# Attention weights of block b+1 beside the values of block b, and the softmax division after P V

## The chip, the cores and the metric

The kernel runs on one core of one Trainium2 chip. The time is device microseconds of one execution of the whole program, the median of several runs. TensorE appears in the profile as PE (matmuls) and PEld (its weight loads), VectorE as DVE, ScalarE as ACT, GpSimd as POOL, and SyncE's DMA queue as SP. Each engine works through its own list of instructions strictly in order; engines wait for each other on semaphores.

## The reference

Two layers (DEPTH = 2) of a decoder trunk over 512 tokens of width 1024. In each layer a norm feeds one projection whose columns are divided among three mixers (sparse attention, an S5 state space, a Mamba-2 SSD), whose outputs go through one output projection, and then a squared-ReLU MLP of width 4096 follows. The part that the change touches is the end of the attention:

```python
logits = jnp.einsum('bqgrd,bqkgd->bqgrk', qg, k_sel).astype(jnp.float32) * ATTN_SCALE
logits = jnp.where(valid[:, :, None, None, :], logits, -jnp.inf)
p = jax.nn.softmax(logits, axis=-1).astype(v_sel.dtype)
o = jnp.einsum('bqgrk,bqkgd->bqgrd', p, v_sel)
```

There are 8 query heads of width 64 in 2 groups of 4 (each group shares its keys and values), and the queries are taken in 4 blocks of 128. Each query keeps at most 128 keys, chosen by an indexer (512 // 4, `topk`).

## The kernel before

Everything lies as columns of tokens: 128 partitions, 512 tokens or 128 keys along the free dimension. The big products are made from two parts, a high and a low one, with three matmuls each (`mm3`, lines 458 to 460); the weights are cut into `whi` on ACT (L191) and `wlo` on DVE (L192) as they arrive.

A layer has two stages. In `mixers` eight or more generators (streams) run side by side: `trunk_in` (input projection), `keys` (key transposes and indexer scores), `select` (top-k masks), `attention`, two `recurrent` streams (S5 and SSD), and three `out_proj` streams (S5's, then attention's, then SSD's part of the output projection). `merge` advances the stream whose own clock is lowest; each `yield` tells how much the step adds to that clock, and tables in `PLAN` scale these steps (`pace`), delay a stream's start (`start`), add to its priority (`prio`) and name the PSUM pool of each tile (`bank`: `m` and `a`, four banks each). The order in which the instructions then stand on each engine is made by the scheduler of the tile framework from these priorities and from buffers as they come free. In `mlp` the second stage runs, nearly alone.

The names that matter, with the lines of the profile:

- `attention` (from L1305) goes through the blocks b = 0 to 3. For each it turns the queries (`rope_q`), splits and transposes them (`hhl` L1042/1043, `hTp` L1046, `hT` L1048), waits for the block's mask, and runs `attend`.
- `attend` (from L1092) makes, for each of 8 heads, the scores `lg` on PE (L1055), the masked scores and their row minimum on DVE (`pe`, `nmax`, L1107), and the exponential with its row sum on ACT (L1108). After four heads it takes the reciprocal of the four sums (L1111) and multiplies each of the four weight tiles by it: head 0 on ACT (L1115, since `norm_act` is (0,)), the other three on DVE (L1117). Then, for each block of keys, four weight tiles of a group are transposed on PE (`pTp`, L1123), copied out of PSUM by ACT (`pT`, L1125) and multiplied by the values (`po`, L1128, 64 output partitions for each group). At the end the four rows of `po` are cut into `mh` (ACT, L1132) and `ml` (DVE, L1133), the operands of the output projection.
- A block's 8 heads and all of its transposes and products with the values are done before the next block's queries are touched.
- Around it run the SSD's steps: `xb` (L1210), the convolution `cv` (L844 to 851), `CT` (L857/858), `ssdT` (L880), `ssds` (L893), `ssdy` (L907/909), `st` (L914), and top-k's `mx`/`isc` (L1086/1087) with the mask's last step (L1090).

Of the kernel before, what the change touches and what calls it, by code (L numbers as in the profile page):

```python
# [10 lines left out]
F32 = mybir.dt.float32  # L11
F32R = mybir.dt.float32r
I32 = mybir.dt.int32
AF = mybir.ActivationFunctionType
ALU = mybir.AluOpType
# [3 lines left out]
P = 128  # L19
# [3 lines left out]
NB = S // P  # L23
# [24 lines left out]
    "serial": "no",  # L48
    "norm_act": (),
    "tab_dve": (),  # L50
# [3 lines left out]
    "prio": {},  # L54
# [9 lines left out]
        "serial": "no",  # L64
        "norm_act": (0,),
        "tab_dve": ("B1", "C2"),
        "pace": {"w": 0.29, "key": 2.007, "idx": 0.686, "top": 0.061, "q": 3.616, "att": 1.702, "s5": 0.084, "ssd": 2.496, "out": 1.504, "tab": 0.3},
        "start": {"tab": 0.5, "key": 5.0, "top": 41.0, "att": 0.0, "s5": 12.0, "ssd": -7.0, "out": 20.0},
        "prio": {"att": 300, "idx": -30, "top": -300, "ssd": 300, "tab": -30, "w": 30, "s5": 30, "out": -30, "q": -300},
        "bank": {"w_kv": "m", "w_qi": "m", "w_q": "m", "w_u5": "m", "w_xa": "a", "w_xb": "m", "w_z": "m", "kT": "a", "hT": "a", "ix": "a", "lg": "a", "pT": "m", "po": "a", "sB": "m", "sst": "a", "sU": "a", "sv": "m", "sy": "m", "st": "m", "sg": "a", "dds": "a", "dseg": "m", "darow": "m", "dT": "a", "ds": "a", "dy": "a", "dst": "a", "dn": "a", "db": "m"},  # L70
    },
# [4 lines left out]
        "serial": "no",  # L76
        "norm_act": (0,),
        "tab_dve": (),
        "pace": {"w": 0.344, "key": 1.011, "idx": 1.036, "top": 0.873, "q": 3.741, "att": 1.652, "s5": 0.357, "ssd": 1.82, "out": 0.453, "tab": 0.853},
        "start": {"tab": 0.0, "key": 0.0, "top": 15.0, "att": -20.0, "s5": -30.0, "ssd": 3.0, "out": 22.0},  # L80
        "prio": {"tab": -30, "out": -100, "att": 1000, "q": -300, "idx": -30, "s5": 1000, "top": -100},
        "bank": {"w_kv": "m", "w_qi": "m", "w_q": "m", "w_u5": "m", "w_xa": "a", "w_xb": "m", "w_z": "m", "kT": "a", "hT": "a", "ix": "b", "lg": "a", "pT": "a", "po": "a", "sB": "m", "sst": "a", "sU": "m", "sv": "m", "sy": "a", "st": "b", "sg": "a", "dds": "a", "dseg": "m", "darow": "m", "dT": "m", "ds": "m", "dy": "a", "dst": "a", "dn": "a", "db": "m"},
    },
# [137 lines left out]
class Net:  # L221
# [869 lines left out]

    def attend(self, b, qT, K, mask, nrs, ah, al):  # L1092

        nc = self.nc
        v = nc.vector
        nk = (b + 1) * P
        po = self.ps(self.bank["po"], (P, 4, P), name="po")
        es = []
        for g_ in range(2):
            sm = self.s([P, 4], tag="psum", bufs=4)  # L1100
            for r in range(4):
                p = self.ps(self.bank["lg"], name="lg")[:, :nk]
                self.head_dot(p, qT[2 * r + g_], K, g_, nk)
                e = self.g(name="pe")[:, :nk]
                nm = self.s([P, 1], tag="nmax", bufs=8)
                h = 2 * r + g_
                v.tensor_tensor_reduce(e, p, mask, nrs[:, h:h + 1], 3.0e38, ALU.add, ALU.min, nm)  # L1107
                nc.scalar.activation(e, e, AF.Exp, bias=nm, scale=-1.0, accum_out=sm[:, r:r + 1])  # L1108
                es.append(e)
                yield self.pace["att"] * (0.4 + 0.25 * b)  # L1110
            v.reciprocal(sm, sm)  # L1111
            for r in range(4):
                e = es[4 * g_ + r]
                if r in self.plan["norm_act"]:
                    nc.scalar.activation(e, e, AF.Copy, scale=sm[:, r:r + 1])  # L1115
                else:
                    v.tensor_scalar(e, e, sm[:, r:r + 1], None, ALU.mult)  # L1117
        for kb in range(b + 1):
            pts = []
            for g_ in range(2):  # L1120
                p = self.ps(self.bank["pT"], (P, 4, P), name="pTp")
                for r in range(4):
                    nc.tensor.transpose(p[:, r], es[4 * g_ + r][:, kb * P:(kb + 1) * P], self.ident)  # L1123
                pt = self.g([P, 4, P], name="pT")
                nc.scalar.activation(pt, p, AF.Copy)  # L1125
                pts.append(pt)
            for g_ in range(2):
                nc.tensor.matmul(po[g_ * 64:g_ * 64 + 64], self.vt[:, kb, g_], pts[g_], start=kb == 0, stop=kb == b)  # L1128
            yield self.pace["att"] * 2.2
        bs = slice(b * P, (b + 1) * P)  # L1130
        for r in range(4):
            nc.scalar.activation(ah[r][:, bs], po[:, r], AF.Copy)  # L1132
            v.tensor_tensor(al[r][:, bs], po[:, r], ah[r][:, bs].bitcast(F32), ALU.subtract)  # L1133

# [170 lines left out]
    def attention(self, l, r):  # L1305
        nc = self.nc
# [3 lines left out]
        q, rt = r["q"], self.rt  # L1310
# [8 lines left out]
        al = [self.g(dt=F32R, name="ml") for _ in range(4)]  # L1319
        for b in range(NB):  # L1320
            self.rope_q(q[b], *rt[2][b])
            qT = self.transpose_heads(q[b])
            yield self.pace["q"] * 2.5
            while b not in r["mask"]:
                yield None
            yield from self.attend(b, qT, r["K"], r["mask"][b], qrs[:, b], ah, al)
        for i in range(4):
# [254 lines left out]
```

## Time and profile before

| | us |
|---|---|
| median of 3 runs | 1332.54 (1331.55 to 1332.56) |
| the profiled execution | 1328.87 |
| its span in the trace | 1327.1 |
| PE busy | 1218.0 (92%) |
| DVE busy | 885.2 (67%) |
| ACT busy | 549.2 (41%) |
| layer 0, mixers / MLP | 0 to about 340 / 340 to 708 |
| layer 1, mixers / MLP | 708 to about 986 / 986 to 1327 |

The blocks of attention run between about 140 and 295 us (layer 0) and between about 842 and 935 us (layer 1). A busy PE in this profile is not a PE at its peak, and PEclk is the clock that was granted, as a share of full speed (1.0 is 2.4 GHz, 0.5 is 1.2 GHz). In a wait that ends for several reasons, the profile names the last one.

### The profile page before, as it was taken

How to read it: one execution, taken by the hardware profiler on the slowest of the kernel's cores; microseconds unless marked ns; L12 is line 12 of the kernel's file. 1: busy time of each engine (PE TensorE's matmuls, PEld its weight loads, DVE VectorE, ACT ScalarE, POOL GpSimd, SP SyncE). 2: the span in 40 equal slices, each digit the busy share in tenths (PEclk: the TensorE clock that was granted, in tenths of full speed). 3: DMA queues.
4: the chain of work that ended last, by engine and by line, in shares of the span. 5: the costliest groups of instructions: out<-in, count | busy, mean ns of one | idle time of the engine just before them, and what ended most of it. 6: DMA issues, size and time to landing. Idle time of an engine off the chain costs nothing.

```text
span 1327.1 us, 17056 instructions
## 1 busy us (share of the span) xinstructions
PE 1218.0 (92%) x5708; PEld 977.1 (74%) x5708; DVE 885.2 (67%) x2024; ACT 549.2 (41%) x1128; POOL 169.7 (13%) x302
## 2 busy tenths in 40 slices
PE   5678957889999989999999989968999999999998
PEld 5566745458888868888888767754788888888887
DVE  5998999857886545665564699975475445444443
ACT  4245444664543533534443234455254233242331
POOL 2385100000796040000000000000000000000000
PEclk9889988899999999999999989978999999999999
DMA  5132220002567647677644634300323333333332
GB/s 189 40 88 70 74 74 24 9 1 72 148 213 257 214 146 252 224 262 230 227 149 137 219 120 124 120 17 1 111 88 97 101 97 96 96 96 99 100 110 81
DMA packets 139688, 161.64 MB, mean 122 GB/s; under 512 B 18768, under 2 KB 107600, under 8 KB 139600
## 3 DMA queue, kind: packets, MB, share of 16 engines
q1 hardware_dynamic: 139600, 160.55, 38.5%
q8 instruction: 45, 0.74, 0.2%
q14 instruction: 43, 0.35, 0.1%
HBM read 128.29 MB, written 31.03 MB: 120 GB/s over the span
## 4 chain that ended last, share of the span: by engine, by line
PE 62%; DVE 19%; issue 7%; POOL 6%; ACT 4%; DMA 1%; SPq 0%; ACTq 0%; DVEq 0%; POOLq 0%
PE pm L458 18%; PE pm L460 18%; PE pm L459 18%; PE po L1128 3%; DVE isc L1087 2%; DVE mx L1086 2%; DVE isc L1076 2%; PE pTp L1123 1%; DVE pe L1107 1%; DVE wlo L192 1%; DMA wraw<-in_w_in_dram 1%; POOL pt L660 1%; DVE cv L847 1%; ACT pe L1108 1%; POOL pt L661 1%
## 5 line engine op out<-in xcount | busy, mean ns | idle before, releaser
L192 DVE TENSOR_TENSOR wlo<-wraw,whi 128x512 fp32r<-128x512 f32 (+1 forms) x312 | 223.2, 718 | 243.0 <-ACT whi L191 241.4
L191 ACT ACTIVATE whi<-wraw 128x512 fp32r<-128x512 f32 (+1 forms) x312 | 194.1, 625 | 374.5 <-PE pm L459 236.9
L458 PE MATMUL pm<-xh,whi 128*128 128x512 f32 x640 | 252.4, 395 | 3.8 <-ACT q L1224 3.2
L460 PE MATMUL pm<-xh,wlo 128*128 128x512 f32 x640 | 250.1, 392 | 1.2 <-DVE wlo L192 1.2
L459 PE MATMUL pm<-xl,whi 128*128 128x512 f32 x640 | 250.9, 392 | 0.0
L460 PE MATMUL pm<-uh,wlo 128*128 128x512 f32 x512 | 199.7, 390 | 0.3 <-DVE wlo L192 0.3
L458 PE MATMUL pm<-uh,whi 128*128 128x512 f32 x512 | 199.6, 390 | 0.0
L459 PE MATMUL pm<-ul,whi 128*128 128x512 f32 x512 | 199.6, 390 | 0.0
L458 PEld LDWEIGHTS pm<-xh,whi 128*128 128x128 f32 x640 | 120.8, 189 | 30.8 <-ACT q L1224 3.9
L460 PEld LDWEIGHTS pm<-xh,wlo 128*128 128x128 f32 x640 | 120.6, 189 | 27.4 <-DVE wlo L192 2.0
L459 PEld LDWEIGHTS pm<-xl,whi 128*128 128x128 f32 x640 | 121.1, 189 | 24.2 <-issue 0.2
L460 PEld LDWEIGHTS pm<-uh,wlo 128*128 128x128 f32 x512 | 96.2, 188 | 20.8 <-DVE wlo L192 0.9
L459 PEld LDWEIGHTS pm<-ul,whi 128*128 128x128 f32 x512 | 96.3, 188 | 20.4 <-issue 0.4
L458 PEld LDWEIGHTS pm<-uh,whi 128*128 128x128 f32 x512 | 96.2, 188 | 20.3 <-issue 0.4
L458 PE MATMUL pm<-whi,xh 128*128 128x512 f32 (+1 forms) x176 | 67.4, 385 | 14.0 <-ACT xh L392 12.8
L460 PE MATMUL pm<-whi,xl 128*128 128x512 f32 (+1 forms) x176 | 66.6, 380 | 1.3 <-DVE xl L394 1.3
L459 PE MATMUL pm<-wlo,xh 128*128 128x512 f32 (+1 forms) x176 | 67.0, 381 | 0.5 <-DVE wlo L192 0.3
L1408 DVE TENSOR_TENSOR ul<-ur,uh 128x512 fp32r<-128x512 f32 x64 | 48.5, 758 | 21.0 <-ACT uh L1407 21.0
L1406 DVE SCALAR_TENSOR_TENSOR ur<-pm,ur 128x512 f32<-128x512 f32 x64 | 43.9, 686 | 23.0 <-ACT ur L1403 22.7
L1414 DVE TENSOR_TENSOR sq<-pm,r2b 128x512 f32<-128x512 f32 x64 | 44.1, 689 | 17.5 <-PE pm L460 17.5
L1407 ACT ACTIVATE uh<-ur 128x512 fp32r<-128x512 f32 x64 | 39.9, 624 | 30.7 <-DVE ur L1406 30.7
L1087 DVE MATCH_REPLACE8 isc<-mx,isc 128x256 f32<-128x256 f32 (+2 forms) x96 | 51.6, 541 | 0.0
(345 smaller groups left out, 1931.4 us busy)
## 6 DMA issues: line engine op xcount, KB each, us to landing
wraw<-in_w_up_dram SPq DMA_DIRECT2D x128, 256.0 KB, 2.8
wraw<-in_w_down_dram SPq DMA_DIRECT2D x128, 256.0 KB, 2.8
st<-shi SPq DMA_DIRECT2D x48, 256.0 KB, 2.9
st<-slo SPq DMA_DIRECT2D x48, 256.0 KB, 3.5
wlo<-st SPq DMA_DIRECT2D x48, 256.0 KB, 3.0
whi<-st SPq DMA_DIRECT2D x48, 256.0 KB, 2.8
wraw<-in_w_in_dram SPq DMA_DIRECT2D x32, 256.0 KB, 2.8
sraw<-in_w_in_dram SPq DMA_DIRECT2D x32, 256.0 KB, 3.9
```

What stands on the lines that cost most here:

```text
L191: nc.scalar.activation(hi, raw, AF.Copy)
L192: nc.vector.tensor_tensor(lo, raw, hi.bitcast(F32), ALU.subtract)
L458: nc.tensor.matmul(p, lh, rh, start=first, stop=False)
L459: nc.tensor.matmul(p, lh, rl, start=False, stop=False)
L460: nc.tensor.matmul(p, ll, rh, start=False, stop=last)
L1076: v.scalar_tensor_tensor(acc, r, wi[:, h:h + 1], acc, ALU.mult, ALU.add)
L1087: v.match_replace(acc, m8, acc, SENT)
L1128: nc.tensor.matmul(po[g_ * 64:g_ * 64 + 64], self.vt[:, kb, g_], pts[g_], start=kb == 0, stop=kb == b)
L1406: v.scalar_tensor_tensor(r, p, 0.0, r, ALU.max, ALU.mult)
L1407: nc.scalar.activation(h, r, AF.Copy)
L1408: v.tensor_tensor(lo, r, h.bitcast(F32), ALU.subtract)
L1414: v.tensor_tensor(t, d[1], rb, ALU.mult)
```

## The change

Three things change together.

1. `attend` is cut in two generators. `weights` makes the scores, exponentials and row sums of a block (the sums of all 8 heads now in one tile, 128x8); `values` does the transposes and the products with the values. `attention` starts `values` of block b together with `weights` of block b+1 and advances them in turn, weights first. The queries of block b+1 are turned and transposed before `values` of block b starts.
2. The weights aren't divided by their sums any more: L1111, L1115 and L1117 go (`norm_act` with them). The reciprocals of all 8 sums are taken in one instruction in `values`. Eight matmuls of 128x128 identity columns against the reciprocal, broadcast to 64 columns, write the reciprocals into a PSUM tile `rsb` with the layout of `po` (64 partitions for a group, one row for each r); ACT copies it to `rn`. After the last `po` DVE multiplies `po` by `rn`, a 128x512 instruction.
3. `mh` and `ml` are cut from `rn` in SBUF and not from `po` in PSUM.

`rsb` lies in pool `m` in layer 0 and in pool `a` in layer 1.

```diff
-    def attend(self, b, qT, K, mask, nrs, ah, al):
+    def weights(self, b, qT, K, mask, nrs, es, sm):
 ...
-        po = self.ps(self.bank["po"], (P, 4, P), name="po")
-        es = []
         for g_ in range(2):
-            sm = self.s([P, 4], tag="psum", bufs=4)
             for r in range(4):
 ...
-                nc.scalar.activation(e, e, AF.Exp, bias=nm, scale=-1.0, accum_out=sm[:, r:r + 1])
+                nc.scalar.activation(e, e, AF.Exp, bias=nm, scale=-1.0, accum_out=sm[:, g_, r:r + 1])
                 es.append(e)
                 yield self.pace["att"] * (0.4 + 0.25 * b)
-            v.reciprocal(sm, sm)
-            for r in range(4):
-                e = es[4 * g_ + r]
-                if r in self.plan["norm_act"]:
-                    nc.scalar.activation(e, e, AF.Copy, scale=sm[:, r:r + 1])
-                else:
-                    v.tensor_scalar(e, e, sm[:, r:r + 1], None, ALU.mult)
+
+    def values(self, b, es, sm, ah, al):
+        po = self.ps(self.bank["po"], (P, 4, P), name="po")
+        v.reciprocal(sm, sm)
+        p = self.ps(self.bank["rsb"], (P, 4, P), name="rsb")
+        for r in range(4):
+            for g_ in range(2):
+                nc.tensor.matmul(p[g_ * 64:g_ * 64 + 64, r], sm[:, g_, r:r + 1].to_broadcast([P, 64]), self.ident, start=True, stop=True)
+        rn = self.g([P, 4, P], name="rn")
+        nc.scalar.activation(rn, p, AF.Copy)
         for kb in range(b + 1):
 ...
+        v.tensor_tensor(rn, po, rn, ALU.mult)
         for r in range(4):
-            nc.scalar.activation(ah[r][:, bs], po[:, r], AF.Copy)
-            v.tensor_tensor(al[r][:, bs], po[:, r], ah[r][:, bs].bitcast(F32), ALU.subtract)
+            nc.scalar.activation(ah[r][:, bs], rn[:, r], AF.Copy)
+            v.tensor_tensor(al[r][:, bs], rn[:, r], ah[r][:, bs].bitcast(F32), ALU.subtract)
 ...
-        for b in range(NB):
-            self.rope_q(q[b], *rt[2][b])
-            qT = self.transpose_heads(q[b])
-            yield self.pace["q"] * 2.5
-            while b not in r["mask"]:
-                yield None
-            yield from self.attend(b, qT, r["K"], r["mask"][b], qrs[:, b], ah, al)
+        work = []
+        for b in range(NB + 1):
+            if b < NB:
+                self.rope_q(q[b], *rt[2][b])
+                qT = self.transpose_heads(q[b])
+                yield self.pace["q"] * 2.5
+            first = b < NB
+            while first or work:
+                if first and b in r["mask"]:
+                    first = False
+                    es, sm = [], self.s([P, 2, 4], tag="psum", bufs=2)
+                    work.insert(0, self.weights(b, qT, r["K"], r["mask"][b], qrs[:, b], es, sm))
+                if first and not work:
+                    yield None
+                for g in list(work):
+                    c = next(g, None)
+                    if c is None:
+                        work.remove(g)
+                    else:
+                        yield c
+            if b < NB:
+                work.append(self.values(b, es, sm, ah, al))
```

Since the scheduler sets the order, the code does not tell where the instructions stand. Three places show it. The lines after the change are three lower than before for the same SSD step; the numbers behind names tell buffers apart.

First, PE in layer 0, at the end of the scores of block 1 (`lg`), before:

```order
L1055 MATMUL lg_2545<-kh_766,hT_2330 128x256
L1055 MATMUL lg_2545<-kl_767,hT_2330 128x256
L1123 MATMUL pTp_2557<-cons,pe_2493 128x128
L1123 MATMUL pTp_2557<-cons,pe_2500 128x128
L1123 MATMUL pTp_2557<-cons,pe_2507 128x128
L1123 MATMUL pTp_2557<-cons,pe_2514 128x128
L1128 MATMUL po_2488<-pT_2562,vt_137 64x512
```

and after, where the next block's query transposes (`hTp`) and the eight matmuls for `rsb` come first:

```order
L1052 MATMUL lg_2540<-kh_766,hT_2195 128x256
L1052 MATMUL lg_2540<-kl_767,hT_2195 128x256
L1043 MATMUL hTp_2555<-cons,hhl_2552 128x128 x4
L1116 MATMUL rsb_2599<-cons,psum_2490 64x128 x8
L1124 MATMUL pTp_2610<-cons,pe_2494 128x128
L1124 MATMUL pTp_2610<-cons,pe_2501 128x128
L1124 MATMUL pTp_2610<-cons,pe_2508 128x128
L1124 MATMUL pTp_2610<-cons,pe_2515 128x128
```

The first transposes of the weights now stand behind `rsb`, which needs the sums of all 8 heads; before, they stood behind the first four heads. The other transposes and the `po` of this block follow later, among the scores of block 2.

Second, PE in layer 1, where the first SSD chunk waits for the convolution (`cv`, `CT`), before:

```order
L1128 MATMUL po_8605<-pT_8739,vt_7149 64x512
L1128 MATMUL po_8605<-pT_8746,vt_7149 64x512
L869 MATMUL arow_8879<-triur,adtl_7539 128x128
L880 MATMUL ssdT_8929<-cons,cv_7635 128x128
L880 MATMUL ssdT_8929<-cons,cv_7978 128x128
L880 MATMUL ssdT_8929<-cons,cv_8788 128x128
L893 MATMUL ssds_8939<-CT_8871,cv_8788 128x128
L1046 MATMUL hTp_8912<-cons,hhl_8909 128x128 x4
```

and after:

```order
L455 MATMUL pm_8839<-mh_8269,whi_8759 128x512
L456 MATMUL pm_8839<-ml_8270,whi_8759 128x512
L457 MATMUL pm_8839<-mh_8269,wlo_8760 128x512
L877 MATMUL ssdT_8916<-cons,cv_8779 128x128
L890 MATMUL ssds_8942<-CT_8862,cv_8779 128x128
L1129 MATMUL po_8887<-pT_8905,vt_7157 64x512
L1129 MATMUL po_8887<-pT_8912,vt_7157 64x512
L1124 MATMUL pTp_8925<-cons,pe_8619 128x128
L1124 MATMUL pTp_8925<-cons,pe_8626 128x128
```

The four products of block 1 with the values stood ahead of the SSD's wait and now stand behind it, while the query transposes of block 2 have moved ahead of it.

Third, DVE in layer 1, the convolution on that chain, before:

```order
L1090 TENSOR_SCALAR isc_7853<-isc_7853 128x512
L1210 TENSOR_TENSOR xb_8766<-pm_8694,rb_7490 128x512
L844 TENSOR_SCALAR cv_8788<-xb_8766,hconvw,hconvb 128x512
L847 SCALAR_TENSOR_TENSOR cv_8788<-xb_8766,hconvw,cv_8788 128x511
L1133 TENSOR_TENSOR ml_8457<-po_8605,mh_8453 128x128
L847 SCALAR_TENSOR_TENSOR cv_8788<-xb_8766,hconvw,cv_8788 128x510
L1133 TENSOR_TENSOR ml_8458<-po_8605,mh_8454 128x128
L847 SCALAR_TENSOR_TENSOR cv_8788<-xb_8766,hconvw,cv_8788 128x509
L1133 TENSOR_TENSOR ml_8459<-po_8605,mh_8455 128x128
L1210 TENSOR_TENSOR xb_8862<-pm_8701,rb_7490 128x512
```

and after:

```order
L1391 TENSOR_TENSOR x_117<-x_117,pm_8831 128x512
L1212 TENSOR_TENSOR xb_8757<-pm_8701,rb_7498 128x512
L841 TENSOR_SCALAR cv_8779<-xb_8757,hconvw,hconvb 128x512
L844 SCALAR_TENSOR_TENSOR cv_8779<-xb_8757,hconvw,cv_8779 128x511
L844 SCALAR_TENSOR_TENSOR cv_8779<-xb_8757,hconvw,cv_8779 128x510
L844 SCALAR_TENSOR_TENSOR cv_8779<-xb_8757,hconvw,cv_8779 128x509
L1212 TENSOR_TENSOR xb_8853<-pm_8708,rb_7498 128x512
L848 SCALAR_TENSOR_TENSOR cv_8779<-cth_8784,cv_8779 128x512
L841 TENSOR_SCALAR cv_8855<-xb_8853,hconvw,hconvb 128x512
L1391 TENSOR_TENSOR x_123<-x_123,pm_8839 128x512
```

The `ml` of block 1, which wait for PE's `po`, no longer stand inside the convolution; its eighth residual sum (`x_123`) does.

## Rows read from the trace of the kernel before

**Rows 1.** The page, part 1: busy time, share of the span, instructions.

```profile
PE 1218.0 (92%) x5708; PEld 977.1 (74%) x5708; DVE 885.2 (67%) x2024; ACT 549.2 (41%) x1128; POOL 169.7 (13%) x302
```

**Rows 2.** Busy time by stretch: length, PE, PEld, DVE, ACT, POOL, PEclk, DMA, GB/s.

```profile
193.00:227.00 34.00, 23.60 (x107) 17.70 (x103) 30.54 (x66) 12.04 (x24) 0.00 (x0) 0.85 0.00 0
227.00:295.00 68.00, 56.34 (x295) 34.98 (x293) 49.41 (x149) 44.18 (x120) 0.00 (x0) 0.92 0.05 16
836.00:887.00 51.00, 41.55 (x203) 30.04 (x201) 42.89 (x140) 24.93 (x76) 0.00 (x0) 0.88 0.25 80
887.00:936.00 49.00, 41.03 (x217) 25.74 (x216) 27.81 (x85) 29.65 (x77) 0.00 (x0) 0.92 0.00 1
940.00:986.00 46.00, 46.00 (x219) 38.05 (x217) 30.05 (x55) 16.30 (x28) 0.00 (x0) 1.00 0.38 121
```

**Rows 3.** Waits of PE, 193 to 296 us: total us, times, longest.

```profile
PE pTp L1123 <- ACT pe L1115: 3.9, 4, 1.8
...
PE hTp L1046 <- DVE hhl L1043: 3.0, 3, 1.3
```

**Rows 4.** Waits of PE, 836 to 940 us.

```profile
PE ssds L893 <- DVE CT L858: 4.2, 1, 4.2
PE pTp L1123 <- ACT pe L1115: 3.5, 4, 2.4
PE ssdT L880 <- DVE cv L851: 3.5, 1, 3.5
```

**Rows 5.** Groups of instructions: busy us, mean ns of one, idle before.

```profile
L1414 DVE TENSOR_TENSOR sq<-pm,r2b 128x512 f32<-128x512 f32 x64 | 44.1, 689 | 17.5 <-PE pm L460 17.5
L1125 ACT ACTIVATE pT<-pTp 128x512 f32<-128x512 f32 x40 | 22.7, 598 | 28.0 <-PE pTp L1123 27.9
...
L1117 DVE TENSOR_SCALAR pe<-pe,psum 128x128 f32<-128x128 f32 (+3 forms) x48 | 15.7, 382 | 0.1
...
L1115 ACT ACTIVATE pe<-pe,psum 128x128 f32<-128x128 f32 (+3 forms) x16 | 8.9, 554 | 1.3 <-DVE psum L1111 1.3
```

**Rows 6.** The chain that ended last: start, us, engine, tile, records.

```profile
315.03 1.78 PE bct L428 x16
```

**Rows 7.** Timeline of PE, layer 1: start, us, line, records.

```profile
907.24 0.45 PE L907 MATMUL ssdy<-dec,xd 128*64 128x128 f32 x4
...
908.32 0.70 PE L914 MATMUL st<-xd,btok 128*128 128x256 f32 x2
```

**Rows 8.** Timeline of PE, layer 0; in brackets the idle time before.

```profile
210.95 2.45 PE L1128 MATMUL po<-pT,vt 128*64 128x512 f32 x4 [6.02 <-ACT pT L1125]
...
231.01 0.28 PE L1055 MATMUL lg<-kl,hT 128*128 128x256 f32 x1
233.09 1.12 PE L1123 MATMUL pTp<-cons,pe 128*128 128x128 f32 x4 [1.80 <-ACT pe L1115]
```

**Rows 9.** Timeline of DVE, layer 0 block 1: the reciprocal of the last four sums.

```profile
234.65 0.16 DVE L1111 RECIPROCAL psum<-psum 128x4 f32<-128x4 f32 x1
```

**Rows 10.** Timeline of DVE, layer 1: the convolution's chain.

```profile
867.30 0.68 DVE L1210 TENSOR_TENSOR xb<-pm,rb 128x512 f32<-128x512 f32 x1
...
872.26 0.29 DVE L1133 TENSOR_TENSOR ml<-po,mh 128x128 fp32r<-128x128 f32 x1 [2.91 <-ACT mh L1132]
...
879.84 0.62 DVE L858 SCALAR_TENSOR_TENSOR CT<-cth,cv 64x512 f32<-64x512 f32 x1
```

**Rows 11.** Timeline of PE, layer 1: the wait for that chain, and block 2's scores.

```profile
880.51 0.80 PE L893 MATMUL ssds<-CT,cv 128*128 128x128 f32 x2 [4.16 <-DVE CT L858]
...
886.96 0.88 PE L1055 MATMUL lg<-kh,hT 128*128 128x384 f32 x1
```

**Rows 12.** Busy time by stretch, four us of layer 1; columns as in rows 2.

```profile
884.00:888.00 4.00, 4.00 (x20) 3.38 (x19) 1.95 (x6) 2.29 (x7) 0.00 (x0) 0.50 0.00 0
```

**Rows 13.** Timeline of PE, layer 0: the last product with the values, and the projection.

```profile
293.53 0.59 PE L1128 MATMUL po<-pT,vt 128*64 128x512 f32 x1
...
294.92 0.73 PE L458 MATMUL pm<-mh,whi 128*128 128x512 f32 x2
```

More of the change, by code (lines that the diff above doesn't have):

```diff
@@ L48 @@
     "serial": "no",
-    "norm_act": (),
     "tab_dve": (),
@@ L64 @@
         "serial": "no",
-        "norm_act": (0,),
         "tab_dve": ("B1", "C2"),
@@ L69 @@
         "prio": {"att": 300, "idx": -30, "top": -300, "ssd": 300, "tab": -30, "w": 30, "s5": 30, "out": -30, "q": -300},
-        "bank": {"w_kv": "m", "w_qi": "m", "w_q": "m", "w_u5": "m", "w_xa": "a", "w_xb": "m", "w_z": "m", "kT": "a", "hT": "a", "ix": "a", "lg": "a", "pT": "m", "po": "a", "sB": "m", "sst": "a", "sU": "a", "sv": "m", "sy": "m", "st": "m", "sg": "a", "dds": "a", "dseg": "m", "darow": "m", "dT": "a", "ds": "a", "dy": "a", "dst": "a", "dn": "a", "db": "m"},
+        "bank": {"w_kv": "m", "w_qi": "m", "w_q": "m", "w_u5": "m", "w_xa": "a", "w_xb": "m", "w_z": "m", "kT": "a", "hT": "a", "ix": "a", "lg": "a", "pT": "m", "po": "a", "rsb": "m", "sB": "m", "sst": "a", "sU": "a", "sv": "m", "sy": "m", "st": "m", "sg": "a", "dds": "a", "dseg": "m", "darow": "m", "dT": "a", "ds": "a", "dy": "a", "dst": "a", "dn": "a", "db": "m"},
     },
@@ L76 @@
         "serial": "no",
-        "norm_act": (0,),
         "tab_dve": (),
@@ L81 @@
         "prio": {"tab": -30, "out": -100, "att": 1000, "q": -300, "idx": -30, "s5": 1000, "top": -100},
-        "bank": {"w_kv": "m", "w_qi": "m", "w_q": "m", "w_u5": "m", "w_xa": "a", "w_xb": "m", "w_z": "m", "kT": "a", "hT": "a", "ix": "b", "lg": "a", "pT": "a", "po": "a", "sB": "m", "sst": "a", "sU": "m", "sv": "m", "sy": "a", "st": "b", "sg": "a", "dds": "a", "dseg": "m", "darow": "m", "dT": "m", "ds": "m", "dy": "a", "dst": "a", "dn": "a", "db": "m"},
+        "bank": {"w_kv": "m", "w_qi": "m", "w_q": "m", "w_u5": "m", "w_xa": "a", "w_xb": "m", "w_z": "m", "kT": "a", "hT": "a", "ix": "b", "lg": "a", "pT": "a", "po": "a", "rsb": "a", "sB": "m", "sst": "a", "sU": "m", "sv": "m", "sy": "a", "st": "b", "sg": "a", "dds": "a", "dseg": "m", "darow": "m", "dT": "m", "ds": "m", "dy": "a", "dst": "a", "dn": "a", "db": "m"},
     },
@@ L1107, in attend @@
                 v.tensor_tensor_reduce(e, p, mask, nrs[:, h:h + 1], 3.0e38, ALU.add, ALU.min, nm)
-                nc.scalar.activation(e, e, AF.Exp, bias=nm, scale=-1.0, accum_out=sm[:, r:r + 1])
+                nc.scalar.activation(e, e, AF.Exp, bias=nm, scale=-1.0, accum_out=sm[:, g_, r:r + 1])
                 es.append(e)
                 yield self.pace["att"] * (0.4 + 0.25 * b)
-            v.reciprocal(sm, sm)
-            for r in range(4):
-                e = es[4 * g_ + r]
-                if r in self.plan["norm_act"]:
-                    nc.scalar.activation(e, e, AF.Copy, scale=sm[:, r:r + 1])
-                else:
-                    v.tensor_scalar(e, e, sm[:, r:r + 1], None, ALU.mult)
+    def values(self, b, es, sm, ah, al):
+        nc = self.nc
+        v = nc.vector
+        po = self.ps(self.bank["po"], (P, 4, P), name="po")
[6 more added lines that the diff above has]
+        nc.scalar.activation(rn, p, AF.Copy)
         for kb in range(b + 1):
```

2 rows, old and new, of the table _PLAN are left out of this document.

## The prediction

> **What bounds the kernel now.** I read the page first: PE is busy for 92% of the span [rows 1]. So time can only come from places where PE idles, or runs at less than full clock, and any work added to PE counts unless it falls into such a place. Then the busy time by stretch [rows 2]. From 940 us on PE has no gap (46.00 of 46.00 us), so a us won at the end of attention reaches the end of the program whole. In the four stretches of attention PE idles 34.0 - 23.6 = 10.4, 68.0 - 56.3 = 11.7, 51.0 - 41.5 = 9.5 and 49.0 - 41.0 = 8.0 us, 39.6 us together, and the granted clock there is 0.85, 0.92, 0.88 and 0.92, worth at most 5.1, 5.4, 6.1 and 3.9 us more. DVE nearly fills the first and third of these stretches (30.5 of 34, 42.9 of 51) but not the others.
>
> The waits say why PE idles [rows 3, 4]. The transposes of the weights wait for the last division (`pe` L1115, 3.9 and 3.5 us), the query transposes of the next block wait for DVE's split (`hhl`, 3.0 us), and in layer 1 the SSD's first chunk waits for the convolution (3.5 + 4.2 us). These are latencies of one block's chain, scores to minimum to exponential to sum to division to transposes to product, with little other PE work ready in between. Two blocks side by side supply such work; that is where a gain must come from.
>
> **The division.** It takes 48 instructions from DVE (15.7 us) and 16 from ACT (8.9 us) [rows 5], and 16 reciprocals become 8 (8 x 0.16 = 1.3 us) [rows 9]. It adds, for each of 8 blocks, a 128x512 product from PSUM on DVE, as the 0.689 us row, and a 128x512 copy on ACT, as the 0.598 us row [rows 5]: 5.5 and 4.8 us. Net DVE loses 11.5 us and ACT 4.1 us. Neither counts by itself: both idle beside PE, and what they give back is the shorter chain, counted below as idle time of PE. Without that cover the two new instructions would cost 1.3 us a block.
>
> On PE it adds 64 matmuls in 8 groups, and this counts. The trace has no `rsb`, but two neighbours of 8 matmuls with 128 moving columns: `bct`, the same broadcast into 128 columns, at 1.78 us [rows 6], and `ssdy`, into 64 output partitions with the two halves in turn, at 908.32 - 907.24 = 1.08 us [rows 7]. `rsb` has `ssdy`'s shape and its alternation, so I take 1.08 us, 8.6 us in all; the other end is 8 x 1.78 = 14.2 us. It can't be negative, since it replaces no PE work.
>
> The Trainium skill says of this (TensorEngine Tiling (Array Packing), section Tiling Modes, Key Properties) that different tiles of a divided array work in parallel but that a change of the tiling mode drains the engine. The parallel half alone would make a group half of 1.78 us and the sum 7.1 us; the trace's 1.08 us lies above that half, as entry and exit would have it, and the sum stays with the row.
>
> **The order, stretch by stretch.** No DMA and no POOL instruction is added; SP's queue only shifts by a few places.
>
> *193 to 227 us.* PE stood 6.02 us before `po` of block 0 [rows 8]. That product now stands behind most of the S5 part of the output projection. But the projection needs S5's last `ml`, which DVE, full here, delivers about when that wait ended. I give nothing for it and charge one `rsb`: +1.1 us.
>
> *227 to 295 us.* At stake are 11.7 us of idle time and at most 5.4 us of clock, 17.1. What stays: PE finished block 1's scores at 231.3 and began transposes at 233.09 [rows 8], but `rsb` needs the sums of all 8 heads, whose last reciprocal came at 234.65 [rows 9]. The eight query transposes now between cover 0.5 us, so some 3.0 us of wait stay, and half of the clock loss, 2.7. Blocks 2 and 3 have SSD matmuls as cover: 1 us each. In the tail (block 3's values with no next block) the first `pT` copy is bare, 0.6 us, and the projection that follows 1.4 us after the last `po` began [rows 13] now waits for `rn` (0.69) and `mh` behind it, with the SSD's last chunk behind the same DVE queue: 1.5 us. That leaves 9.8, a gain of 7.3, less three `rsb` (3.2): -4.1 us.
>
> *836 to 887 us.* The chain from `xb` to the first `CT` took 880.46 - 867.30 = 13.2 us on DVE, of which 2.91 us were a wait of `ml` for PE's `po`, and 0.8 the four `ml` themselves, 0.3 an `hhl` [rows 10]. These leave the chain; one residual sum (0.6) comes in: 9.7 us. Its start moves up, since the twelve divisions of blocks 0 and 1 go (at the group's mean of 0.382 us at most 4.6 us [rows 5]; I take 2.7, these being the two smaller shapes) and with them about as many small waits as make 1.5: to about 863. So `CT` is there at about 872.8 instead of 880.5. PE reached the place at 872.0; without block 1's four products and eight transposes (4.4), without 1.0 of waits, with two `rsb` (2.2) and the query transposes (1.0) it comes at about 869.7 and stands 3.1 us. Behind it are then 6.0 us of work before block 2's scores (before: 3.5, which took 886.96 - 880.51 = 6.5 us [rows 11], since PE after 8 us with almost nothing to do ran at 0.50, 1.2 GHz [rows 12]). The shorter stand should cost half of that clock loss, so 9 us: scores of block 2 at about 881.8, -5.2 us with both `rsb` inside.
>
> *887 to 936 us.* 8.0 + 3.9 = 11.9 us at stake. Staying: `rsb` of blocks 2 and 3 (1.0 and 1.5), clock 1.0, bare `pT` 0.6, tail 0.8 (seven of the SSD's eight matmuls stand between here). Gain 7.0, less two `rsb` (2.2): -4.8 us.
>
> Sum: 1.1 - 4.1 - 5.2 - 4.8 = -13.0 us. The profiled execution took 1328.87 us (span 1327.1), 3.7 us under the median of 1332.54; 13.0 us off it is 1315.9, off the median 1319.5. I state the median. Since waits were read off one execution, a measurement can tell about 0.2% (2.7 us) from no change.
>
> **Rivals.**
>
> *`rsb` is a gate* (slower). PE takes its list in order, and `rsb` holds everything behind it until the eighth exponential of the block, where before four were enough. In layer 0's block 1 that is 234.65 + 0.16 - 233.09 = 1.7 us later [rows 8, 9]. My sum holds 7.5 us of such stands (3.0, 1, 1, 1, 1.5), a mean of 0.9 for 8 groups. If the cover is never ready in time and each group stands 3.5 us (1.7 and as much again at half clock behind it), that is 28 us, 20.5 more: about 1340. It decides when the mean stand passes 0.9 + 13.0 / 8 = 2.5 us. For it: PE's in-order wait of 1.80 us there [rows 8]. Against: in five of eight places other matmuls stand directly before `rsb`.
>
> *The idle time is only filled.* The added matmuls take the gaps and the chains end when they did: 1332, within 2.7 us. For it: DVE is full where layer 0's first blocks run [rows 2]. Against: PE, not DVE, has the work at the end of both layers.
>
> *The two blocks hardly overlap.* In layer 1 the new order puts block 1's products behind the SSD's wait, not among block 2's scores, so half of the gains of 7.3 and 7.0 us that rest on overlap is lost, 7.2 us; the earlier `CT` does not depend on it: 1326.7, still faster.
>
> *The clock stays up.* If PE never stands long enough for 1.2 GHz, some 10 us more come: 1308.
>
> **How the numbers follow.** Forecast 1319.5, chance 0.50; little overlap, 0.13; clock up, 0.12 (all faster); filled idle time, 0.10 (same); gate, 0.15 (slower). So faster 0.75, same 0.10, slower 0.15. The low end, 1308: layer 0's stretches give 9 us more and layer 1's last 3. The high end, 1335: `rsb` at 1.78 us (5.6 us more) and half of the gains (9.8 us) are 15.4 us above 1319.5. Outside lie about 0.08 below and 0.11 above.
>
> **What would show it.** `rsb` as 8 groups of about 1.1 us (two records for each matmul). PE's idle time in the attention stretches falling from 39.6 to some 20 us. In layer 1 `xb` to `CT` without `ml` inside and near 10 us long, `ssds` waiting 3 us and not 4.2 after 3.5, and block 2's scores 8 us earlier, counted with what layer 0 won. DVE's busy time down by 11 us, ACT's by 4, PE's up by 8 to 14. Waits of `rsb` for the reciprocal of 3 us in layer 0's block 1 and about 1 elsewhere; if they pass 2.5 us on average, the gate has it. If PE's stretches shorten and the time does not, something behind 940 us has grown that I take to be unchanged.

## The result, and the profile after

The changed kernel takes **1339.15 us** (median of 11 runs, 1333.85 to 1340.79), the kernel before 1331.55 us beside it (11 runs, 1330.54 to 1332.59): ratio 1.0051, 95% interval 1.004 to 1.0062. It is slower by 7.6 us; the forecast was 13 us faster, with 1335 as the high end. Below, a *stand* is idle time of PE ahead of an instruction (the brackets of a timeline give it), and *cover* is other work that fills it.

The page of the changed kernel, its span and part 1 (busy us, share, instructions):

```profile
span 1332.0 us, 17258 instructions
...
PE 1222.8 (92%) x5836; PEld 983.5 (74%) x5836; DVE 876.4 (66%) x1976; ACT 546.2 (41%) x1120; POOL 171.7 (13%) x302
```

Against [rows 1] DVE gives back 8.8 us and ACT 3.0, less than the prediction's 11.5 and 4.1, and PE is busy 4.8 us longer, where 8 to 14 were forecast. The profiled execution (1333.85 us) is the shortest of the eleven: 4.9 us of the 7.6 can be seen in it. The longer ones have a lower mean granted clock: 0.967 in the profiled one, 0.961 to 0.964 in the six above 1339 us.

To place them I cut both traces at the same three instructions: the first `s5yT` of layer 0, and the statistic `ms<-tsum` that opens each MLP and layer 1. The three `ms` on DVE's timeline of the changed kernel (start and length in us, then what is done):

```profile
344.26 0.16 DVE L417 TENSOR_SCALAR ms<-tsum 128x4 f32<-128x4 f32 x1 [0.83 <-PE tsum L415]
714.10 0.16 DVE L417 TENSOR_SCALAR ms<-tsum 128x4 f32<-128x4 f32 x1 [8.35 <-PE tsum L415]
992.05 0.16 DVE L417 TENSOR_SCALAR ms<-tsum 128x4 f32<-128x4 f32 x1 [1.15 <-PE tsum L415]
```

Before, these stood at 339.88, 709.68 and 987.12. The MLPs are the same length in both (369.8 and 340.0 us). So layer 0 loses 4.4 us (it reaches `s5yT` 2.3 us earlier and loses 6.7 from there on) and layer 1's mixers 0.5. Busy time between the cuts, of the kernel before and then of the changed one (columns as in [rows 2]):

```profile
194.26:339.88 145.62, 124.04 (x604) 89.93 (x605) 113.58 (x277) 76.59 (x178) 0.00 (x0) 0.93 0.08 26
709.68:987.12 277.44, 246.79 (x1229) 190.39 (x1229) 207.40 (x610) 121.40 (x299) 0.53 (x1) 0.94 0.31 99
```

```profile
191.94:344.26 152.32, 126.86 (x668) 90.78 (x669) 112.90 (x268) 75.90 (x176) 0.00 (x0) 0.94 0.09 29
714.10:992.05 277.95, 248.32 (x1293) 195.01 (x1293) 202.43 (x587) 119.44 (x295) 0.53 (x1) 0.94 0.31 99
```

The four attention stretches of [rows 2], by the same times of the changed kernel, hold 10.1 + 14.8 + 7.7 + 8.6 = 41.3 us of idle time; 39.6 was to fall to some 20:

```profile
193.00:227.00 34.00, 23.89 (x118) 17.16 (x117) 32.24 (x69) 14.73 (x30) 0.00 (x0) 0.95 0.11 32
227.00:295.00 68.00, 53.17 (x302) 33.20 (x303) 42.81 (x127) 38.37 (x105) 0.00 (x0) 0.90 0.01 5
836.00:887.00 51.00, 43.33 (x231) 32.20 (x229) 43.61 (x133) 23.48 (x69) 0.00 (x0) 0.91 0.26 83
887.00:936.00 49.00, 40.36 (x240) 29.06 (x238) 24.87 (x75) 28.97 (x78) 0.00 (x0) 0.86 0.00 1
```

Between the cuts, in layer 0 PE's idle time grows from 21.6 to 25.5 us where it should have shrunk, and the 64 added records of `rsb` come on top; in layer 1 it stays at 30. The waits of PE, 193 to 300 and 836 to 945 us of the changed kernel (total us, times, longest), against [rows 3, 4]:

```profile
PE hTp L1043 <- DVE hhl L1040: 5.7, 2, 3.0
PE lg L1052 <- ACT btok L883: 5.6, 1, 5.6
...
PE rsb L1116 <- DVE psum L1111: 2.6, 1, 2.6
```

```profile
PE ssds L890 <- DVE CT L855: 4.8, 1, 4.8
...
PE rsb L1116 <- DVE psum L1111: 2.3, 1, 2.3
```

The transposes no longer wait for a division. But PE now waits longer at the next block's query transposes `hTp` (5.7 us in layer 0, before 3.0) and at `rsb`, 4.8 us in two places; ahead of the other six `rsb` it doesn't stand. That is little beside a loss of 20 us against the forecast, so the experiments had to say which half of the change costs what.

### The profile page after: what moved, and what is told of

Its sections match the earlier page's. It is cut to its first block, busy times and chain, and to the rows that moved or that the text cites. A ratio compares the mean times of both kernels' runs of the same rounds, so it can differ in the third digit from the quotient of the medians.

```text
span 1332.0 us, 17258 instructions
## 1 busy us (share of the span) xinstructions
PE 1222.8 (92%) x5836; PEld 983.5 (74%) x5836; DVE 876.4 (66%) x1976; ACT 546.2 (41%) x1120; POOL 171.7 (13%) x302
## 4 chain that ended last, share of the span: by engine, by line
PE 69%; DVE 21%; issue 4%; ACT 4%; DMA 1%; POOL 1%; SPq 0%; ACTq 0%; DVEq 0%; POOLq 0%
PE pm L457 20%; PE pm L456 20%; PE pm L455 20%; PE po L1129 2%; DVE mx L1083 2%; DVE isc L1084 2%; DVE isc L1073 2%; DVE wlo L189 1%; DVE pe L1101 1%; DVE cv L844 1%; PE pTp L1124 1%; ACT pe L1102 1%; DMA wraw<-in_w_in_dram 1%; PE hTp L1043 1%; PE rsb L1116 1%
## 5 line engine op out<-in xcount | busy, mean ns | idle before, releaser
L1426 DVE TENSOR_TENSOR ul<-ur,uh 128x512 fp32r<-128x512 f32 x64 | 47.2, 738 | 21.2 <-ACT uh L1425 21.0
L1432 DVE TENSOR_TENSOR sq<-pm,r2b 128x512 f32<-128x512 f32 x64 | 44.1, 689 | 18.3 <-PE pm L457 18.1
L455 PE MATMUL pm<-mh,whi 128*128 128x512 f32 x128 | 50.0, 400 | 5.2 <-ACT mh L781 2.8
```

Source lines behind the costliest of these rows:

```text
L455: nc.tensor.matmul(p, lh, rh, start=first, stop=False)
L1426: v.tensor_tensor(lo, r, h.bitcast(F32), ALU.subtract)
L1432: v.tensor_tensor(t, d[1], rb, ALU.mult)
```

## Experiments

Theory A: `rsb`, the broadcast of the reciprocals, is what costs. Theory B: the side-by-side order is. Each kernel was timed against the kernel before on the same chip; the difference given is of the two medians (before: 1330.99 to 1332.07 us), the interval that of the ratio.

**1. Each half alone, and `rsb` moved.** The first four kernels:

*Side by side, old division* (in `weights`; no `rsb`, no `rn`):

```
+            v.reciprocal(sm[:, g_], sm[:, g_])
+            for r in range(4): ... e <- e * sm[:, g_, r:r + 1]   (as before, r == 0 on ACT)
-        p = self.ps(self.bank["rsb"], (P, 4, P), name="rsb")
...
-        v.tensor_tensor(rn, po, rn, ALU.mult)
```

> The weights of block b+1 beside the values of block b, as in the changed kernel, but each weight is divided by its sum before the transposes, as in the kernel before: no rsb, no rn. Theory A (the broadcast product rsb costs the time: 8 x 1.08 us of PE work, and the transposes stand behind it until the last sum of a block): without it the kernel is faster than before, by 4 to 10 us, 1322 to 1328. Theory B (the order itself costs: scores of b+1 are slowed by the products of b, and the last block's values and the SSD's last chunk come later): it is no faster than before, 1331 to 1338, although PE has 8.6 us less to do than in the changed kernel.

Measured: 1336.74 us, +5.0 (1.003 to 1.006). Theory B is borne out: the order alone makes the kernel slower.

*Late division, blocks one after the other:*

```
+        for b in range(NB): ... yield from self.weights(b, ...)
+            yield from self.values(b, es, sm, ah, al)
```

> The blocks one after the other, as in the kernel before, with only the division moved behind P V: rsb, rn and the product are there, the two blocks are not side by side. Theory A: slower than before by what rsb costs without cover, 5 to 9 us, 1337 to 1341, at least as slow as the changed kernel (1339). Theory B: the shorter chain pays for rsb, 1330 to 1335, faster than the changed kernel by 4 us or more.

Measured: 1336.04 us, +4.3 (1.0024 to 1.0049), between the two ranges, 1 us under theory A's and 1 us above theory B's; theory A also had it at least as slow as the changed kernel, and it is 3.1 us faster. Still it is slower than the kernel before: each half is a loss by itself.

*Side by side, `rsb` late:* the same lines of `rsb` and `rn`, moved between the last transposes and the last product of the block:

```
         for kb in range(b + 1):
             ... transposes, copies pT
+            if kb == b:
+                rsb (8 matmuls), rn <- rsb
             ... products po
```

> The changed kernel with rsb and the copy rn behind the last transposes of the block and ahead of its last product, so that no transpose stands behind the broadcast and it lies where PE waits for the copies pT. Theory A (rsb is a gate): the waits of PE for the reciprocal (4.8 us in two places) go and the clock behind them comes back, 1331 to 1335. Theory B: within 2 us of the changed kernel, 1337 to 1341, since the same matmuls are issued and the order of the two blocks is the same.

Measured: 1319.84 us, **-11.9** (0.9907 to 0.9933). Moving the same instructions by a few lines is worth 19 us, far more than theory A said; theory B expected nothing.

*`rsb` in its first place, from a constant:*

```
-  sm[:, g_, r:r + 1].to_broadcast([P, 64]), self.ident
+  self.con("ones")[:, r:r + 1].to_broadcast([P, 64]), self.ident
```

> The changed kernel with rsb fed from a constant column and not from the reciprocals of the sums, so that the division is left out of what is computed; the same matmuls, copies and products run, but nothing waits for the sums. It prices the wait alone. Theory A: 1329 to 1334, 5 to 10 us under the changed kernel. Theory B: 1336 to 1340, at most 3 us under it.

Measured: 1329.40 us, -2.3 (0.9976 to 1.0002): 9.9 us of the 19.5 are the wait for the sums. How so, when PE's recorded waits at `rsb` are 4.8 us? The order that is written for PE tells it. Layer 0, block 1, from the changed kernel (-) to the one with the constant (+); each `pTp` row is one head's transpose:

```
+L1124 MATMUL pTp_2610<-cons,pe_2494 128x128
 L1052 MATMUL lg_2526<-kh_766,hT_2185 128x256
...
+L1124 MATMUL pTp_2610<-cons,pe_2501 128x128
 L1052 MATMUL lg_2540<-kh_766,hT_2195 128x256
 L1052 MATMUL lg_2540<-kl_767,hT_2195 128x256
-L1043 MATMUL hTp_2555<-cons,hhl_2552 128x128 x4
-L1116 MATMUL rsb_2599<-cons,psum_2490 64x128 x8
-L1124 MATMUL pTp_2610<-cons,pe_2494 128x128
-L1124 MATMUL pTp_2610<-cons,pe_2501 128x128
 L1124 MATMUL pTp_2610<-cons,pe_2508 128x128
```

With `rsb` first all transposes of a block are listed behind the last of its eight sums. Without the wait they go one by one between the scores, each as its exponential comes. The late division makes this possible, since a transposed weight needs no sum any more; `rsb` in front took it away again.

**2. What is left of each half once `rsb` is late.** Theory C: transposes free of the sums are the gain, and the other block's work beside them is needed for it.

*`rsb` late, blocks one after the other* (edits 2 and 3 together):

> The division behind P V with rsb in the late place (behind the last transposes, 1319.8 us side by side), but the blocks one after the other, as in the kernel before. Theory C (two things are needed: transposes that wait for no sum, and another block's work beside them): slower than side by side with rsb late by 3 to 10 us, 1323 to 1330. Rival (side by side gives nothing; the whole gain is the shorter chain of one block): 1318 to 1322.

Measured: 1311.96 us, **-19.4** (0.9836 to 0.9871). The fastest kernel of the study, and below both ends: theory C falls in its second half. The late division needs no neighbour; side by side costs 7.5 us on top of it. DVE's lighter load is not what gains: the kernel with `rsb` first, serial, has the same instructions on DVE and is slower than before (+4.3). PE in this kernel, block 1 of layer 0 (timeline):

```profile
232.14 0.28 PE L1052 MATMUL lg<-kl,hT 128*128 128x256 f32 x1
232.50 0.33 PE L1118 MATMUL pTp<-cons,pe 128*128 128x128 f32 x1
...
233.27 0.28 PE L1052 MATMUL lg<-kl,hT 128*128 128x256 f32 x1
233.47 0.33 PE L1118 MATMUL pTp<-cons,pe 128*128 128x128 f32 x1
...
236.41 1.61 PE L1130 MATMUL po<-pT,vt 128*64 128x512 f32 x4
```

and in the changed kernel, the same block:

```profile
234.53 1.12 PE L1043 MATMUL hTp<-cons,hhl 128*128 128x128 f32 x4 [2.68 <-DVE hhl L1040]
235.57 1.98 PE L1116 MATMUL rsb<-cons,psum 128*64 128x128 f32 x16
...
237.48 1.13 PE L1124 MATMUL pTp<-cons,pe 128*128 128x128 f32 x8
...
243.30 1.07 PE L1129 MATMUL po<-pT,vt 128*64 128x512 f32 x2
```

Counted from `s5yT` (193.93 and 191.94), the first product of block 1 comes at 42.5 us in the one and 51.4 in the other.

*`rsb` late and from a constant* (side by side):

> rsb in the late place and fed from a constant column, so that the division is left out of what is computed and nothing of PE waits for a sum. Theory C: in the late place the sums are long there, so this is within 1.5 us of the same kernel with the sums (1319.8): 1318 to 1321. Rival (rsb is still a gate there): 1315 or less.

Measured: 1321.00 us, -10.4 (0.9907 to 0.9941), no faster than with the sums (-11.9). In the late place no wait for them can be told from the noise.

*`rsb` in the other PSUM ring* (`"rsb": "a"` in layer 0, `"m"` in layer 1):

> The changed kernel (rsb first) with rsb's PSUM tile in the other ring: a in layer 0, m in layer 1. It asks whether the 9.6 us that the first place costs even without a wait (1329.4 against 1319.8) are PSUM buffers that rsb holds while it stands. If so: 1330 to 1335. If it is the place in PE's and ACT's list: within 2.5 us of 1339.

Measured: 1340.72 us, +9.3 (1.006 to 1.0101). The other ring does not help. A shortage that either ring would have is not excluded by this run; how long the buffer is held is tried in part 5.

*`rsb` second*, `if kb == 0:` in place of `if kb == b:`

> rsb and rn behind the transposes of the first key block of each block, ahead of its first product, instead of behind the last transposes. Theory C (what counts is that the transposes don't stand behind the sums): 1318 to 1323. Rival D (what counts is the cover that rsb gives to the last copies pT, at the end of the block): blocks 1 to 3 lose it, 1326 to 1332.

Measured: 1327.99 us, -3.4 (0.9965 to 0.999): 8.5 us worse than late. Rival D's number. Blocks 1 to 3 have the transposes of further key blocks and all products behind it, so it can be a gate again for these. Whether the 8.5 us are the wait or the lost cover of the last copies, the time alone does not part; the end of part 5 comes back to it.

**3. Why side by side costs.** In the changed code the rotation and the head transposes `hTp` of block b+1 are issued ahead of the values of block b (theory F); or it is the products between the scores (rival G).

*One key block of the values ahead of the heads* (side by side, `rsb` late):

```
                 work.append(self.values(b, es, sm, ah, al))
+                yield next(work[0])
```

> Side by side with rsb late (1319.8 us), but the first key block of block b's values is issued ahead of the rotation and the head transposes hTp of block b+1; only the rest runs beside the next scores. Theory F (side by side costs because the values of b stand behind the head transposes of b+1, which wait for DVE's split hhl): most of the 7.9 us to the serial order (1312.0) comes back, 1312 to 1315.5. Rival G (it costs because products of b are put between the scores of b+1 and so delay the next block's chain): 1317.5 to 1321.

Measured: 1317.01 us, -14.0 (0.9881 to 0.9907): 2.1 of the 7.5 us come back, less than theory F said and nearer rival G's range (1317.5 to 1321). Only the first of up to four key blocks was moved.

*Serial, but the heads of b+1 ahead of the values of b* (`rsb` late):

```
+        for b in range(NB + 1):
+            rope_q, transpose_heads of b
+            if b: yield from self.values(b - 1, es, sm, ah, al)
+            yield from self.weights(b, ...)
```

> The serial order with rsb late (1312.0 us), but the rotation and the head transposes of block b+1 are issued ahead of block b's values; scores and values don't alternate. Theory F: it loses what side by side loses, 1317 to 1321. Rival G: within 2 us of 1312, or faster, since the next block's query is then ready early.

Measured: 1323.54 us, -7.5 (0.9931 to 0.9957), slower still than theory F said. The heads ahead cost 11.9 us by themselves, more than side by side as a whole (7.5). So it is the place of the heads that costs, as theory F has it, and not G's alternation, which gives back some 4 us: -11.9 with it, -7.5 without. The first product of block 1 comes 52.1 us after `s5yT` here, again 10 us late. That it costs through the wait for `hhl`, as F says, is not shown: PE stands 4.0 us for it in layer 0 and 0.8 in layer 1 here, and 4.9 and 1.4 in the serial order with `rsb` late. Between the cuts of both layers PE idles 5.0 us more than there, and the same records are busy 5.9 us longer.

**4. The price of the added matmuls.**

*Each `rsb` issued twice* (serial, late; `for r in [0, 1, 2, 3] * 2:`):

> The serial order with rsb late, with the 8 matmuls of each rsb issued twice into the same tile: 8 x 1.09 = 8.7 us of PE work more and nothing else. It prices the added PE work where it stands best. If none of it is covered: 1320.7. If PE's waits for the last copies pT (0.2 to 0.9 us a block) take it: 1314 to 1318.

Measured: 1323.65 us, -7.3 (0.9925 to 0.9951): 12.1 us dearer than once, 1.5 us a group. None of it is covered: PE idles 45.0 us between the cuts, against 44.1. The 3.4 us above the 8.7 go with a lower granted clock (0.92 and 0.95 in the two layers, against 0.96 and 0.96), so 1.5 us is not the price of a group alone.

**5. Wait and place.** Open was the first place itself: side by side 9.9 us are the wait, and the constant still lost 8.1 us by standing first (-2.3 against -10.4).

> The serial order with rsb in the first place (1336.0 us with the sums, 1312.0 in the late place), fed from a constant column, so that the division is left out of what is computed and nothing waits for a sum. It splits those 24 us into the wait for the sums and the place itself. If the wait is most of it: 1312 to 1318. If the place is, as 8.4 us of it were side by side (1329.4 against 1321.0): 1319 to 1325. If neither wait nor place alone explains it: over 1328.

Measured: 1313.42 us, -18.7 (0.9847 to 0.9874). In the serial order the place costs 0.7 us, less than the noise, and the wait 23.0 of the 23.7 (+4.3 to -18.7).

*The copy `rn` moved behind the last `pT`* (side by side, first, constant):

> Side by side with rsb first and fed from the constant column (1329.4 us; division left out), but the copy rn stands in ACT's list behind the last copies pT and not ahead of the first. It asks what the first place costs without a wait. If it is ACT's 0.6 us a block ahead of the copies pT: 1321 to 1325. If it is PE's work ahead of the transposes, or a PSUM buffer held longer: 1328 to 1334.

Measured: 1329.15 us, -2.9 (0.9973 to 0.9991): not ACT's copy either, and not how long `rsb` holds its PSUM buffer, which it now holds until the last copy `pT` is done. The 8.1 us of the place exist only side by side; where they lie, the end of this part takes up.

*`rsb` behind the last product* (serial):

> The serial order with rsb and rn behind the last product of the block instead of ahead of it. If the late place is good because the transposes are free of it, this is within 2.5 us of 1312.0, but for the end of each layer, where rn (0.6 us) and the product then come later: 1312 to 1316. If it is good because rsb fills PE's wait for the last copies pT (0.6 to 0.9 us in each of 8 blocks): 1316 to 1320.

Measured: 1328.59 us, -3.5 (0.9966 to 0.9988): 15.9 us worse than ahead of the last product, beyond both expectations. The granted clock differs. Layer 0, eight us that hold the second group of query transposes of block 2 and then of block 3, first with `rsb` last, then with `rsb` late (the number behind POOL's is the granted clock; 1.00 is 2.4 GHz throughout, 0.57 nearly all at 1.2 GHz):

```profile
242.76:250.76 8.00, 6.67 (x29) 5.70 (x30) 6.29 (x20) 4.66 (x14) 0.00 (x0) 0.57 0.00 0
266.76:274.76 8.00, 7.09 (x25) 6.04 (x25) 5.33 (x14) 4.88 (x14) 0.00 (x0) 0.57 0.00 0
```

```profile
241.93:249.93 8.00, 6.43 (x35) 5.20 (x35) 6.55 (x21) 4.75 (x14) 0.00 (x0) 0.79 0.00 0
263.93:271.93 8.00, 6.05 (x39) 4.43 (x37) 6.27 (x19) 5.92 (x17) 0.00 (x0) 1.00 0.00 0
```

and the stands around them, PE's timeline, `rsb` last and then late:

```profile
241.70 0.66 PE L1043 MATMUL hTp<-cons,hhl 128*128 128x128 f32 x4 [0.72 <-DVE hhl L1040]
244.09 1.12 PE L1043 MATMUL hTp<-cons,hhl 128*128 128x128 f32 x4 [1.74 <-DVE hhl L1040]
...
265.47 0.66 PE L1043 MATMUL hTp<-cons,hhl 128*128 128x128 f32 x4 [0.71 <-DVE hhl L1040]
267.67 1.09 PE L1043 MATMUL hTp<-cons,hhl 128*128 128x128 f32 x4 [1.54 <-DVE hhl L1040]
```

```profile
241.76 0.66 PE L1043 MATMUL hTp<-cons,hhl 128*128 128x128 f32 x4 [0.41 <-DVE hhl L1040]
...
244.16 1.11 PE L1043 MATMUL hTp<-cons,hhl 128*128 128x128 f32 x4 [1.57 <-DVE hhl L1040]
...
263.68 0.66 PE L1043 MATMUL hTp<-cons,hhl 128*128 128x128 f32 x4 [0.30 <-DVE hhl L1040]
...
265.88 0.63 PE L1043 MATMUL hTp<-cons,hhl 128*128 128x128 f32 x4 [1.48 <-DVE hhl L1040]
```

In each pair the stands differ by half a us. Those of 2.46 and 2.25 us go with 0.57, that of 1.98 with 0.79 and that of 1.78 with 1.00; the second `hTp` take 1.1 us at the lower clock and 0.63 at the full one. These places are not all of it: 226.76 to 234.76 us have 0.62 with `rsb` last, and eight us at the same work (229.93 to 237.93) 1.00 with `rsb` late. Over layer 0's stretch the kernel with `rsb` last idles 18.7 us and the other 17.4, but the same 668 matmul records are busy 128.42 and 122.19 us; layer 1 has the same picture. `rsb` last, and then late:

```profile
190.76:337.83 147.07, 128.42 (x668) 98.12 (x669) 113.45 (x269) 75.02 (x176) 0.00 (x0) 0.90 0.10 31
708.34:984.81 276.47, 248.14 (x1293) 194.03 (x1293) 202.24 (x586) 119.12 (x295) 0.53 (x1) 0.94 0.32 100
```

```profile
193.93:333.49 139.56, 122.19 (x668) 90.16 (x669) 111.44 (x265) 74.80 (x176) 0.00 (x0) 0.96 0.10 30
703.47:971.63 268.16, 241.47 (x1293) 190.71 (x1293) 201.71 (x586) 119.16 (x295) 0.53 (x1) 0.96 0.33 102
```

In both layers together PE idles 2.9 us more with `rsb` last and is busy 12.9 us longer with the same records: most of the loss goes with the lower clock. What makes it fall is open.

The same split says something of the two open questions, the first place without a wait and `rsb` second. Side by side, `rsb` first from a constant, and then `rsb` late:

```profile
192.45:340.26 147.81, 128.45 (x668) 92.83 (x669) 112.72 (x268) 75.43 (x176) 0.00 (x0) 0.92 0.10 30
710.23:988.84 278.61, 250.79 (x1293) 196.68 (x1293) 202.52 (x587) 119.14 (x295) 0.52 (x1) 0.93 0.32 99
```

```profile
192.37:332.63 140.26, 122.58 (x668) 90.40 (x669) 111.60 (x265) 75.63 (x176) 0.00 (x0) 0.95 0.09 29
703.73:977.06 273.33, 243.57 (x1293) 191.42 (x1293) 201.74 (x587) 118.84 (x295) 0.52 (x1) 0.95 0.32 101
```

PE idles as long in both (47.2 and 47.4 us), and the same records are busy 13.1 us longer in the first: where nothing waits, the loss by the first place shows as longer busy time at a lower clock and not as idle time. With `rsb` second it is alike (46.9 us idle, 378.5 busy, clock 0.91 and 0.93), so neither more wait nor less cover is to be seen there. The wait itself does show as idle time: from `rsb` first with the sums to `rsb` first from a constant it falls by 7.9 us side by side and by 16.3 in the serial order. Each of these is one execution of each kernel, and why the clock is lower in some no run settles.

All of it together, in us against the kernel before:

| | old division | `rsb` first | `rsb` late |
|---|---|---|---|
| one block after the other | 0 | +4.3 | -19.4 |
| side by side | +5.0 | +7.6 (the change) | -11.9 |

## Why the prediction was wrong

**The sign, and the rival.** The change was forecast at -13.0 us and measured at +7.6. The rival "`rsb` is a gate" gave 1340; it had 0.15 and was right in sign. That its time is within 1 us is in part luck: its 28 us of stands at `rsb` were not there, and its test was not met. PE stands 4.8 us at eight `rsb`, 0.6 each and not 2.5. What is right in it is that the transposes stand behind the sums; that wait is worth 9.9 us side by side. The order for PE is written with the wait known, so transposes and products are listed later, and the loss shows as other waits and as a later end. "In five of eight places other matmuls stand directly before `rsb`" was true and no argument: in the trace five of them are query transposes of the next block, which had been put ahead of the block's own work. And part of the loss is not that rival's: the table gives +5.0 for the order and +2.6 for the division, or, taken the other way round, +4.3 for the division and +3.3 for the order.

**The price of `rsb`.** Sized at 1.08 us a group from `ssdy` [rows 7]; a group is that long:

```profile
215.89 1.09 PE L1116 MATMUL rsb<-cons,psum 128*64 128x128 f32 x16
...
902.10 1.98 PE L1116 MATMUL rsb<-cons,psum 128*64 128x128 f32 x16
```

At half clock (0.50 from 902.10 to 904.08) it is 1.98. Doubling it cost 12.1 us and not 8.6, some of that by the clock (part 4), still under the far end of 14.2. By the half price, an estimate worked out from what the Trainium skill says of tiles that work in parallel (TensorEngine Tiling (Array Packing), section Tiling Modes, Key Properties), it would have been 7.1 us, 0.89 a group; the 1.09 us of a group speak against it.

**193 to 227 us.** Forecast +1.1 and no gain, since DVE is full. Block 1's last score comes at 231.43, before at 231.01: +0.4. A stand nearly as long as the 6.02 us of [rows 8] is there again, but ahead of a score of block 1 and not of the projection:

```profile
229.34 0.58 PE L1052 MATMUL lg<-kh,hT 128*128 128x256 f32 x1 [5.55 <-ACT btok L883]
```

**227 to 295 us.** Forecast -4.1; from block 1's last score to the MLP it is 112.8 us against 108.9, +4.0 (PE idles 14.8 us in this stretch, before 11.7). The step that failed is "The eight query transposes now between cover 0.5 us". They were counted as cover; PE waits at them for `hhl` on DVE (2.68 us above, 2.99 in the next block), and `rsb` and the values of the block stand behind. Heads ahead of the values cost 11.9 us in the serial order with `rsb` late; how much of the 4.0 us here is this wait is not shown. The second failing is that only stands at `rsb` were counted as staying. Block 3's products then ended 2.6 us later (before 293.53 + 0.59 [rows 13]), and the SSD's last `ssds`, which had stood among them at 281.29, came behind them:

```profile
294.93 1.83 PE L1129 MATMUL po<-pT,vt 128*64 128x512 f32 x4
...
296.69 0.71 PE L890 MATMUL ssds<-CT,cv 128*128 128x128 f32 x4
```

**836 to 887 us.** Right in sign, half in size. `xb` to `CT` was to fall from 13.2 to 9.7 us; from `xb` to the `ssds` that waits for `CT` it is 880.79 - 870.55 = 10.2:

```profile
870.55 0.68 DVE L1212 TENSOR_TENSOR xb<-pm,rb 128x512 f32<-128x512 f32 x1
```

```profile
880.79 0.79 PE L890 MATMUL ssds<-CT,cv 128*128 128x128 f32 x2 [4.78 <-DVE CT L855]
...
888.70 0.53 PE L1052 MATMUL lg<-kh,hT 128*128 128x384 f32 x1
```

The term that failed is its start: counted from the layer's `ms`, `xb` comes 156.5 us in, before 157.6, so 1.1 earlier and not 4.3. PE stands 4.8 + 0.8 us in place of 3.1, and block 2's scores come 2.7 us earlier in the layer, not 5.2.

**887 to 936 us.** Forecast -4.8; from block 2's scores to the MLP it is 103.4 us against 100.2, +3.2. Of the 7.0 us to be had from two blocks beside each other nothing came: the first product of block 2 (906.01) is 191.9 us into the layer, before 186.5 (896.20), and the granted clock of the stretch is 0.86, before 0.92.

0.4 + 4.0 - 2.7 + 3.2 = 4.9 us, what the two spans differ by.

**The reading under it.** "Two blocks side by side supply such work; that is where a gain must come from" is the sentence that was wrong. The waits of [rows 3, 4] name the division, and the late division alone, with `rsb` out of the transposes' way, is worth 19.4 us: it takes the serial order's idle time from 21.6 to 17.4 us in layer 0 and from 30.7 to 26.7 in layer 1, and the clock there from 0.93 and 0.94 to 0.96. That is 8.2 us less idle time, and 7.2 us less busy time in spite of 128 records more: nearly half of what the two traces differ by goes with the clock. The prediction put both halves into one sum of idle time to be had, and so did not ask what each would do alone. That the forecast of 1319.5 is within 0.4 us of the side-by-side kernel with `rsb` late is no support for its sum, since that rests on other terms.

## What to carry to other kernels

When a division is moved behind a product, its reciprocals and their broadcast do not belong at the head of the stage: in PE's list, which is worked through in order, the transposes behind it then wait for its operand. Nor is the very end a safe place. Here one place, between the last transposes and the last product, was 8 to 24 us better than the places before and behind it, so try several. Of a change with two halves, forecast each alone, and count among what is moved ahead (here the next block's heads) every instruction that waits for another engine.

## What the runs showed of the hardware that was not expected

Half a us more of standing went with several times as much loss. Around four `hTp` of layer 0, stands of 2.46 and 2.25 us went with a granted clock of 0.57 over eight us, a stand of 1.98 us with 0.79 and one of 1.78 us with 1.00; a layer with 1.3 us more idle time had 6.2 us more busy time for the same matmuls (128.42 against 122.19 us). Why these stands differ in effect no run settles, since the work ahead of them differs too. The clock also goes with the spread within one kernel: of the changed kernel's eleven executions, 1333.85 to 1340.79 us, the six above 1339 us have a mean granted clock of 0.961 to 0.964, the five below of 0.966 to 0.969.
